# Loading and adding the expert rows of a mixture-of-experts block ahead of its last expert, whose own rows come in by a one-hot matmul

## The chip, the cores and the metric

The kernel runs on one core of a Trainium2 chip. Its time is the device time of one execution in microseconds (us). A profile of one execution stands beside it: its span runs from the first instruction to the last, and the execution's own time is a little longer.

## The reference, cut to what matters

One encoder layer: attention and pooling, an output projection, then a mixture of experts over 1024 tokens of 1024 channels, then a final norm. Each token goes to two of 32 experts, and its output is the weighted sum of their two rows.

```python
xb = x_pad[row_tok].reshape(n_blocks, MOE_BLOCK, D)
def expert_block(args):
    xblk, e = args
    hid = jax.nn.silu(xblk @ w_gate[e]) * (xblk @ w_up[e])
    return hid @ w_down[e]
yb = lax.map(expert_block, (xb, block_e)).reshape(P, D)
y = jnp.zeros((N + 1, D), jnp.float32).at[row_tok].add(yb.astype(jnp.float32) * row_w[:, None])
...
x = x + g2[:, None] * y
return rms_norm(x, final_g)
```

## The kernel before

Attention, projection, second norm and router come first; the router leaves, for every expert, up to 128 slots: `ix[:, 0, e]` holds the token of each slot, `ix[:, 1, e]` its row in a DRAM array `yd` of 2048 rows (two for each token), `LV[:, e]` its weight. Slots that no token took carry an index out of bounds and move nothing. Where an expert has more than 128 tokens, a loop under `tc.If(nr > 0)` takes the rest in further rounds; on these inputs `nr` is 0 and the loop's body is not entered.

The main loop walks over `seq`, 384 steps of one 512 KB weight tile (`we`) each. A tile is split four steps ahead (`AHEAD`) into a rounded part `wh`, written by ScalarE (ACT), and the rest `wl`, written by VectorE (DVE); PE multiplies with three products each. For expert `e`, GpSimd (POOL) gathers the tokens' rows by an indirect DMA, PE transposes them (`px`), ACT and DVE split them into `xs`; `pg` holds the gate and up products, `hx` the hidden rows, `pht` and `hth` their transpose, `py` the result. ACT evicts `py` with the weights as `y`, and POOL scatters `y` into `yd`. An expert's down products stand between the gate and up products of the next, so the last expert's end has nothing beside it.

After the loop comes the If, and after it the tail: `g2B` (the gate row, broadcast) is loaded, then 16 loads of 512 KB bring `yd` back as `fy{t}_0` and `fy{t}_1` for the eight token tiles `t`. Per tile, PE adds the two by multiplying both with the identity into `yp`; DVE multiplies with `g2B` and adds the residual `xf`; ACT squares and sums; DVE and POOL make the factor `frs`; DVE scales with `frs` and the norm's row `fgB`; and SyncE (SP) stores the tile.

The engines run their instructions in program order (`pins`). All large tiles are slabs of 4 KB a partition out of one pool of 50 (`slab`, tag "s"); a slab that is given back goes to a later tile, and what writes that tile first waits for the last use of the slab by its former owner. A ring (`ring`) takes its slabs when each of its tiles is first asked for, and keeps them. SP's loads go out in order, and each waits for the semaphore that the load eight before it raises on landing (`DMAHW0` to `DMAHW7`); POOL's have `DMASW0` to `DMASW7`.

At the If every engine that goes past the body first waits, in the branch not taken, until its own semaphores stand where the program left them before the If, and then sets them to what the body would have left. For SP these are the eight semaphores of its loads.

Of the kernel before, what the change touches and what calls it, by code (L numbers as in the profile page):

```python
# [9 lines left out]
F32 = mybir.dt.float32  # L10
# [58 lines left out]
def block_kernel(ctx: ExitStack, tc: tile.TileContext, A):  # L69
# [32 lines left out]
    def dma(dst, src):  # L102
        tc.keep_in_program_order(nc.sync.dma_start(dst, src))  # L103
# [4 lines left out]
    def pool_dma(dst, src):  # L108
        tc.keep_in_program_order(nc.gpsimd.dma_start(dst, src))
# [82 lines left out]
    xnd = dram.tile([S, D], F32, name="xnd")  # L192
    mvd = dram.tile([T, P, 2, 3, NE], F32, name="mvd")
    LV = cst.tile([P, NE], F32, name="LV")
    ix = cst.tile([P, 2, NE], I32, name="ix")

    seq = []
# [13 lines left out]
    with tc.tile_pool(name="ps0", bufs=2, space=PSUM) as psum, tc.tile_pool(name="ps1", bufs=2, space=PSUM) as psum1, \  # L211
# [9 lines left out]
        def pw(name, shape):  # L221
            return shaped(psum1.tile([P, 512], F32, name=name, tag="w"), shape)
# [19 lines left out]
        def w_split(m, eng=None):  # L242
            w = wsp[m]
            hi, lo = slab(f"wih{m}", (KD, P), F32R), slab(f"wil{m}", (KD, P), F32R)
            split(w, hi, lo, eng)
            wsp[m] = hi, lo
# [785 lines left out]

        dve.tensor_scalar(ix, lists[:, 0:64].rearrange("p (a b) -> p a b", a=2), FAR, None, op0=OP.add)
        dve.tensor_copy(LV, lists[:, 64:96])
        pn = pw("pn", (NE,))
        pe.matmul(pn, ones_b, cums[:, T], start=True, stop=True)
        most = cst.tile([P, 2], F32, name="most")
# [12 lines left out]
    with tc.tile_pool(name="ps5", bufs=2, space=PSUM) as psum, tc.tile_pool(name="ps6", bufs=4, space=PSUM) as psum1:  # L1050

        def pt(name):
            return psum.tile([P, 1024], F32, name=name, tag="p")

        def pq(name, shape=(512,)):
            t = psum1.tile([P, 512], F32, name=name, tag="q")[:, :int(np.prod(shape))]
            if len(shape) == 2:
                t = t.rearrange("p (a b) -> p a b", a=shape[0])
            return t

        def gather(dst, col):
            pool.indirect_dma_start(
                out=dst, out_offset=None, in_=xnd,
                in_offset=bass.IndirectOffsetOnAxis(ap=col, axis=0), bounds_check=S - 1, oob_is_err=False)

        SC = []

        def scatter(src, col):
            s = pool.indirect_dma_start(
                out=yd, out_offset=bass.IndirectOffsetOnAxis(ap=col, axis=0), in_=src, in_offset=None,  # L1070
                bounds_check=2 * S - 1, oob_is_err=False)
            for o in SC:
                tc.declare_no_dep(s.ins, o.ins, reason="each row is written once")
            SC.append(s)

        XF = []
        XT, PG, PU, HS, HT, PY = {}, {}, {}, {}, {}, {}
        RINGS = {}
        XG = [X2.pop(t) for t in (T - 2, T - 1)]
        X2.clear()  # L1080

        def ring(name, n, shape=(1024,), dt=F32):

            r = RINGS.setdefault(name, [[], 0])
            if len(r[0]) < n:
                r[0].append(slab(f"{name}{len(r[0])}", shape, dt))
            r[1] += 1
            return r[0][(r[1] - 1) % n]

        def w_split(e, i):  # L1090
            if i < 8 + DOWN:
                w = RW[e, i]
                hi, lo = ring("wh", WQ, dt=F32R), ring("wl", WQ, dt=F32R)
                split(w, hi, lo)
                RW[e, i] = hi, lo

        PX = {}

        def make_x(e, step):

            a, second = divmod(step, 2)
            if not second:
                p = PX[a] = pq(f"px{e}_{a}", (4, P))
                for b in range(4):
                    k = 4 * a + b
                    pe.transpose(p[:, b], XG[e % 2][:, k * P:(k + 1) * P], ident)
            else:
                x = XT[e, a] = ring("xs", 3, (2, 4, P), F32R)
                split(PX.pop(a), x[:, 0], x[:, 1])

        def products(e, i):
            w, RW[e, i] = RW[e, i], None
            if i < 8:
                hi, lo = w
                if i % 4 == 0:
                    (PG, PU)[i // 4][e] = pq(f"pg{e}_{i}")
                p = (PG, PU)[i // 4][e]
                for j in range(2):
                    k, cs = 2 * (i % 4) + j, slice(j * 512, (j + 1) * 512)
                    x = XT[e, k // 4]  # L1120
                    mm3(p, x[:, 0, k % 4], x[:, 1, k % 4], hi[:, cs], lo[:, cs], k == 0, k == KD - 1)
            else:
                k = i - 8
                if k == 0:
                    PY[e] = pt(f"py{e}")
                for h in range(2):
                    cs = slice(h * 512, (h + 1) * 512)
                    if k < DOWN:
                        mm3(PY[e][:, cs], HT[e][0][:, 0, k], HT[e][0][:, 1, k], w[0][:, cs], w[1][:, cs], k == 0, k == KF - 1)
                    else:  # L1130
                        pe.matmul(PY[e][:, cs], HT[e][1][:, k], w[:, cs], start=(k == 0), stop=(k == KF - 1))

        def hidden(e):
            dve.tensor_tensor(HS[e], HS[e], PU.pop(e), op=OP.mult)

        def hidden_t(e):
            hs = HS.pop(e)
            p = pq(f"pht{e}", (KF, P))
            for k in range(KF):
                pe.transpose(p[:, k], hs[:, k * P:(k + 1) * P], ident)  # L1140
            HT[e] = ring("hth", 1, (2, DOWN, P), F32R), DOWN < KF and ring("ht", 1, (KF, P))
            split(p[:, :DOWN], HT[e][0][:, 0], HT[e][0][:, 1])
            if DOWN < KF:
                act.activation(HT[e][1][:, DOWN:], p[:, DOWN:], AF.Copy)

        gather(XG[0], ix[:, 0, 0:1])
        gather(XG[1], ix[:, 0, 1:2])
        pool_dma(*stores.pop())
        for g in range(AHEAD):
            w_split(*seq[g])  # L1150
        for step in (0, 2, 1, 3):
            make_x(0, step)
        for g, (e, i) in enumerate(seq):
            while len(RW) < min(g + 1 + LOAD, len(seq)):
                w_next()
            if len(RW) == len(seq) and not XF:
                for t in range(T):
                    XF.append(slab(f"xf{t}"))
                    dma(XF[t], x2d[t * P:(t + 1) * P])
            if g + AHEAD < len(seq):  # L1160
                w_split(*seq[g + AHEAD])
            products(e, i)
            if i >= 8:
                e += 1
            j = i + 4 * (4 <= i < 8) - 4 * (i >= 8)
            if j == 0:
                if e > 0:
                    hidden(e - 1)
                if e + 2 < NE:
                    gather(XG[e % 2], ix[:, 0, e + 2:e + 3])  # L1170
            if j == HTJ and 0 < e < NE:
                hidden_t(e - 1)
            if j == 4 - (e == 0) and e < NE:
                HS[e] = ring("hx", 1, (512,))
                act.activation(HS[e], PG.pop(e), AF.Silu)
            if j == 8 and e > 0 or j == 7 and e == NE:
                y = ring("y", YN)
                act.activation(y, PY.pop(e - 1), AF.Copy, scale=LV[:, e - 1:e])
                scatter(y, ix[:, 1, e - 1:e])
            if j == 11 and e == NE - 1:  # L1180
                hidden(e)
                hidden_t(e)
            if e + 1 < NE and j in (X_AT if e else X_AT0):
                make_x(e + 1, (X_AT if e else X_AT0)[j])


    nr = nc.values_load(nri[0:1, 0:1], min_val=0, max_val=7)
    with tc.tile_pool(name="ps7", bufs=1, space=PSUM) as psum:
        with tc.If(nr > 0):
            with tc.For_i(0, nr):  # L1190
# [14 lines left out]
                with tc.For_i(0, NE) as e:  # L1205
# [33 lines left out]
                                             start=(k == 0), stop=(k == KF - 1))  # L1239
                    nc.scalar.activation(y, py.rearrange("p a b -> p (a b)"), AF.Copy, scale=wc)  # L1240
                    scatter(y, col[:, 1])


    g2B = slab("g2B")
    bcast_row(g2B, rowd[3:4], D)
    Y = []
    for t in range(T):
        for k in range(2):
            Y.append(slab(f"fy{t}_{k}"))
            dma(Y[-1], yd.rearrange("(t k) d -> k t d", k=2)[k, t * P:(t + 1) * P])  # L1250

    pins.update(EN)
    psum = ctx.enter_context(tc.tile_pool(name="ps8", bufs=3, space=PSUM))
    fgB = rows(psum.tile([P, D], F32, name="fgB", bufs=1), fg)
    SS, RF, YP = {}, {}, {}
    for t in range(-1, T + 2):
        if t + 1 < T:
            y0, y1 = Y[2 * t + 2:2 * t + 4]
            p = YP[t + 1] = psum.tile([P, 2, 512], F32, name=f"yp{t + 1}", tag="yp")
            for h in range(2):  # L1260
                for i, y in enumerate((y0, y1)):
                    pe.matmul(p[:, h], ident, y[:, h * 512:(h + 1) * 512], start=(i == 0), stop=(i == 1))
        if 0 <= t < T:
            y0, y1 = Y[2 * t:2 * t + 2]
            dve.tensor_tensor(y0, YP.pop(t).rearrange("p a b -> p (a b)"), g2B, op=OP.mult)
# [93 lines left out]
```

## Time and profile before

| | |
|---|---|
| time, median of 3 runs | 1163.71 us (1161.6 to 1164.07) |
| the profiled execution: its own time | 1163.77 us |
| its span | 1162.0 us |
| busy over the span | PE 94%, DVE 83%, ACT 63%, POOL 21% |
| mean granted clock of TensorE | 0.97 of full speed |

The busy shares are means over stages with different limits: the expert loop runs from about 537 to 1110 us, the tail from 1110 us on. Lines of the profile name the place in the program; a helper that records the operations gives nearly all of them line 82, so tiles are named instead. A row of the timeline gives start, duration, engine, line, operation, output<-inputs and, in brackets, how long the engine had been idle and what ended that.

### The profile page before, as it was taken

What the parts mean: (1) busy time and instruction counts of PE and PEld (TensorE: products, weight loads), DVE (VectorE), ACT (ScalarE), POOL (GpSimd) and SP (SyncE); (2) the same over time, 40 slices, a digit from 0 to 9 for tenths busy, and PEclk for the clock granted to TensorE, in tenths of its full rate; (3) what the DMA queues carried; (4) which work ended last, traced back from release to release, by engine and by line L of the source; (5) the groups of instructions that cost most, each with busy time, mean ns of one, the idle gap of its engine ahead of it and who ended that gap; (6) DMA issues with size and microseconds to landing.
All of it is one profiled execution on the core that took longest, in us unless ns stands there. A gap on an engine that the chain in (4) does not pass through costs nothing.

```text
span 1162.0 us, 15763 instructions
## 1 busy us (share of the span) xinstructions
PE 1094.0 (94%) x5319; PEld 894.8 (77%) x5319; DVE 967.5 (83%) x1222; ACT 726.8 (63%) x931; POOL 242.7 (21%) x195
## 2 busy tenths in 40 slices
PE   5998998999999999878999999999999999999975
PEld 5787786779888877777888888888888888888742
DVE  6977787589998247997999999999999999999827
ACT  6641232388887001216888888888888888888712
POOL 1000000168888001541011011110110110110001
PEclk8899999999999999969999999999999999999988
DMA  9949699696837853774999999999999999999155
GB/s 368 374 148 379 215 341 339 254 262 150 198 113 248 332 199 129 246 273 142 337 374 387 386 382 394 382 388 391 383 389 381 389 384 386 380 388 344 39 222 222
DMA packets 103718, 349.61 MB, mean 301 GB/s; under 512 B 16754, under 2 KB 17682, under 8 KB 103634
## 3 DMA queue, kind: packets, MB, share of 16 engines
q1 hardware_dynamic: 92034, 323.08, 76.4%
q0 software_dynamic: 11456, 24.96, 5.7%
q8 instruction: 43, 0.70, 0.2%
q10 hardware_dynamic: 144, 0.52, 0.1%
q14 instruction: 41, 0.34, 0.1%
HBM read 309.95 MB, written 55.33 MB: 314 GB/s over the span
## 4 chain that ended last, share of the span: by engine, by line
issue 46%; PE 27%; DVE 12%; POOL 6%; DMA 6%; ACT 1%; SPq 1%; POOLq 0%; DVEq 0%; ACTq 0%
PE pm L82 6%; PE s L82 4%; PE po L82 4%; POOL x L82 4%; PE pz_v L82 3%; PE pz_u L82 3%; POOL yd L82 2%; PE pw L82 2%; DVE rt L82 2%; DVE wt L82 2%; DMA k<-kd 1%; DVE fy L82 1%; SPq L103 1%; PE yp L82 1%; PE pz_q L82 1%
## 5 line engine op out<-in xcount | busy, mean ns | idle before, releaser
L82 DVE TENSOR_TENSOR wl<-we,wh 128x1024 fp32r<-128x1024 f32 x384 | 458.3, 1221 | 39.8 <-ACT wh L82 35.4
L82 ACT ACTIVATE wh<-we 128x1024 fp32r<-128x1024 f32 x384 | 399.7, 1058 | 60.4 <-PE pg L82 29.2
L82 PE MATMUL pg<-wh,xs 128*128 128x512 f32 x1024 | 338.7, 397 | 0.0
L82 PEld LDWEIGHTS pg<-wh,xs 128*128 128x128 f32 x1024 | 192.8, 188 | 39.2 <-ACT xs L82 0.2
L82 PE MATMUL pg<-wl,xs 128*128 128x512 f32 x512 | 200.1, 391 | 0.0
L82 PE MATMUL py<-wh,hth 128*128 128x512 f32 x512 | 171.8, 397 | 1.0 <-ACT hth L82 0.7
L82 POOL DMA_INDIRECT yd<-y,ix x32 | 32.2, 1005 | 479.5 <-ACT y L82 466.9
L82 PEld LDWEIGHTS py<-wh,hth 128*128 128x128 f32 x512 | 96.0, 188 | 21.8 <-DVE hth L82 1.2
L82 PEld LDWEIGHTS pg<-wl,xs 128*128 128x128 f32 x512 | 96.7, 189 | 18.3
L82 PE MATMUL py<-wl,hth 128*128 128x512 f32 x256 | 99.8, 390 | 0.0
L82 ACT ACTIVATE e<-s,mx 128x1024 f32<-128x1024 f32 x64 | 71.6, 1119 | 28.9 <-DVE mx L82 25.6
L82 DVE TENSOR_REDUCE mx<-s 128x1 f32<-128x1024 f32 x64 | 78.2, 1222 | 5.9 <-PE s L82 3.2
L82 PE MATMUL s<-k,sq 128*128 128x512 f32 x256 | 72.5, 405 | 5.7 <-ACT e L82 4.6
L82 POOL TENSOR_TENSOR e<-e,e 128x1024 f32<-128x1024 f32 x32 | 76.6, 2393 | 2.7
L82 PE MATMUL po<-wh,v 128*128 128x256 f32 x256 | 60.6, 301 | 0.0
L82 DVE SCALAR_TENSOR_TENSOR wt<-wt,cB 128x1024 f32<-128x1024 f32 x48 | 56.3, 1219 | 0.8 <-ACT cB L82 0.8
L82 POOL TENSOR_SCALAR e<-e,cc 128x1024 f32<-128x1024 f32 x32 | 39.3, 1228 | 83.3 <-DVE cc L82 72.2
L82 PEld LDWEIGHTS py<-wl,hth 128*128 128x128 f32 x256 | 48.2, 188 | 9.4
L82 PEld LDWEIGHTS s<-k,sq 128*128 128x128 f32 x256 | 44.0, 189 | 14.5 <-ACT e L82 7.9
L82 ACT ACTIVATE xn<-x 128x1024 f32<-128x1024 f32 x7 | 7.4, 1062 | 75.3 <-DVE x L82 64.7
L82 POOL DMA_INDIRECT x<-xnd,ix x32 | 46.2, 1442 | 35.5 <-PE px L82 13.8
L82 PE MATMUL pm<-woB,mxh 128*128 128x512 f32 x128 | 44.5, 430 | 4.4 <-DVE x L82 4.4
(236 smaller groups left out, 1842.5 us busy)
## 6 DMA issues: line engine op xcount, KB each, us to landing
we<-in_w_exp SPq DMA_DIRECT2D x384, 512.0 KB
wt<-in_w_ada SPq DMA_DIRECT2D x48, 512.0 KB
win<-in_w_in SPq DMA_DIRECT2D x16, 512.0 KB
woB<-wod SPq DMA_DIRECT2D x16, 512.0 KB
fy<-yd SPq DMA_DIRECT2D x16, 512.0 KB
k<-kd SPq DMA_DIRECT2D x32, 192.0 KB
xt<-in_xT SPq DMA_DIRECT2D x8, 512.0 KB
wo<-in_w_out SPq DMA_DIRECT2D x8, 512.0 KB
```

What stands on the lines that cost most here:

```text
L82: ins = getattr(self.eng, op)(*args, **kw)
L103: tc.keep_in_program_order(nc.sync.dma_start(dst, src))
```

## The change

The last expert's rows no longer go through `yd`. Near the start of the expert loop POOL clears a slab (`zero`) and scatters it into the last expert's rows of `yd`. The 16 loads of `yd` are issued inside the loop, during the last expert's up products, behind the scatter of the last expert but one, and DVE adds the two rows of a token tile (`first_sum`): three tiles before the last expert's down products in program order, five in the tail. POOL makes a one-hot `OH` of 128 slots by 1024 tokens, and PE adds `OH` times the last `y` to the identity product of the sum. In the If's body the loads and three sums are made again. `g2B` is still loaded after the If.

```diff
+        dve.tensor_scalar(tlast, lists[:, NE - 1:NE], FAR, None, op0=OP.add)
...
+        def sums_load(h):
+
+            t, k = divmod(h, 2)
+            if len(Y) < 2 * T:
+                Y.append(slab(f"fy{t}_{k}"))
+            dma(Y[h], yd.rearrange("(t k) d -> k t d", k=2)[k, t * P:(t + 1) * P])
+
+        def first_sum(t):
+            dve.tensor_tensor(Y[2 * t], Y[2 * t], Y[2 * t + 1], op=OP.add)
+
         gather(XG[0], ix[:, 0, 0:1])
         gather(XG[1], ix[:, 0, 1:2])
         pool_dma(*stores.pop())
+        zero = slab("zero")
+        pool.memset(zero, 0.0)
+        scatter(zero, ix[:, 1, NE - 1:NE])
+        del zero
...
+            if i == 8 and e == NE - 1:
+                for t in range(3):
+                    first_sum(t)
...
-                scatter(y, ix[:, 1, e - 1:e])
+                if e < NE:
+                    scatter(y, ix[:, 1, e - 1:e])
+                else:
+                    ylast = y
+            if j == 9 and e == NE - 1:
+
+                OH.append(slab("onehot"))
+                pool.iota(OH[0], pattern=[[1, S]], base=0, channel_multiplier=0, allow_small_or_imprecise_dtypes=True)
+                pool.tensor_scalar(OH[0], OH[0], tlast, None, op0=OP.is_equal)
+                for h in range(2 * T):
+                    sums_load(h)
...
     g2B = slab("g2B")
     bcast_row(g2B, rowd[3:4], D)
-    Y = []
-    for t in range(T):
-        for k in range(2):
-            Y.append(slab(f"fy{t}_{k}"))
-            dma(Y[-1], yd.rearrange("(t k) d -> k t d", k=2)[k, t * P:(t + 1) * P])
...
     for t in range(-1, T + 2):
+        if 3 <= t + 2 < T:
+            first_sum(t + 2)
         if t + 1 < T:
-            y0, y1 = Y[2 * t + 2:2 * t + 4]
             p = YP[t + 1] = psum.tile([P, 2, 512], F32, name=f"yp{t + 1}", tag="yp")
             for h in range(2):
-                for i, y in enumerate((y0, y1)):
-                    pe.matmul(p[:, h], ident, y[:, h * 512:(h + 1) * 512], start=(i == 0), stop=(i == 1))
+                cs = slice(h * 512, (h + 1) * 512)
+                pe.matmul(p[:, h], ident, Y[2 * t + 2][:, cs], start=True, stop=False)
+                pe.matmul(p[:, h], OH[0][:, (t + 1) * P:(t + 2) * P], ylast[:, cs], start=False, stop=True)
```

How the instructions move is shown at three places. The first is ACT at the start of the expert loop, where it writes the first rounded weights and the first rounded token rows (`xs0`, `xs1`; the numbers behind the names count tiles, and brackets give the semaphores waited for). Before:

```order
L82 ACTIVATE wh0_4709<-we0_0_3960 128x1024 [waits DMAHW4_49,DMAHW3_49]
L82 ACTIVATE wh1_4713<-we0_1_3962 128x1024 [waits DMAHW5_49,DMASW6_49,Pool_49]
L82 ACTIVATE wh2_4717<-we0_2_3972 128x1024 [waits DMAHW6_49,DVE_49,Activation_49]
L82 ACTIVATE wh3_4721<-we0_3_3974 128x1024 [waits DMAHW0_49,DMAHW7_49,DMASW0_49,PE_49]
L82 ACTIVATE xs0_4735<-px0_0_4725 128x512 [waits DVE_49,PE_49]
L82 ACTIVATE xs1_4738<-px0_1_4730 128x512 [waits DVE_49,PE_49]
L82 ACTIVATE wh4_4741<-we0_4_3984 128x1024 [waits DVE_49]
```

And with the change:

```order
L82 ACTIVATE wh0_4716<-we0_0_3961 128x1024 [waits DMAHW5_49,DMAHW4_49,Pool_49]
L82 ACTIVATE wh1_4720<-we0_1_3963 128x1024 [waits DMAHW2_49,Activation_49]
L82 ACTIVATE wh2_4724<-we0_2_3973 128x1024 [waits DMAHW1_49,DMAHW6_49,DVE_49,PE_49]
L82 ACTIVATE wh3_4728<-we0_3_3975 128x1024 [waits DMAHW7_49,DMASW1_49,Activation_49]
L82 ACTIVATE xs0_4742<-px0_0_4732 128x512 [waits DVE_49,PE_49]
L82 ACTIVATE xs1_4745<-px0_1_4737 128x512 [waits DVE_49,PE_49]
L82 ACTIVATE wh4_4748<-we0_4_3985 128x1024 [waits DMAHW0_49,DVE_49]
```

The order is the same, but `zero` took a slab of the pool, so the rings' tiles fall on other slabs: `wh3` now waits for `DMASW1`, which stands for POOL's store of `mv` to `mvd` (`pool_dma(*stores.pop())`, line 109), the last user of its slab. Before, that wait stood on DVE at `wl4`, behind both `xs`. With the change `wl4` waits for `DMASW3`, the landing of `zero`'s scatter.

The second place is SP from the last `xf` load on. Before, these rows stand behind the If, whose branch not taken ends with the first of them:

```order
L1189 UNCONDITIONAL_BRANCH [waits DMAHW0_49,DMAHW1_49,DMAHW2_49,DMAHW3_49,DMAHW4_49,DMAHW5_49,DMAHW6_49,DMAHW7_49]
L103 DMA g2B_9723<-rowd_115 128x1024 [waits DMAHW1_49,DVE_49]
L103 DMA fy0_0_9725<-yd_117 128x1024 [waits DMASW7_49,DMAHW2_49,DMASW1_49,PE_49]
L103 DMA fy0_1_9727<-yd_117 128x1024 [waits DMAHW3_49,DVE_49]
L103 DMA fy1_0_9729<-yd_117 128x1024 [waits DMAHW4_49,PE_49]
```

With the change, ahead of the If (the first five of the 16 loads) and behind it:

```order
L103 DMA xf7_9274<-x2d_116 128x1024 [waits DMAHW0_49,DMASW5_49,DVE_49]
L103 DMA fy0_0_9509<-yd_117 128x1024 [waits DMAHW1_49,DMASW7_49,DVE_49]
L103 DMA fy0_1_9511<-yd_117 128x1024 [waits DMAHW2_49,DVE_49]
L103 DMA fy1_0_9513<-yd_117 128x1024 [waits DMAHW3_49,DVE_49]
L103 DMA fy1_1_9515<-yd_117 128x1024 [waits DMAHW4_49,DVE_49]
L103 DMA fy2_0_9517<-yd_117 128x1024 [waits DMAHW5_49,DVE_49]
```

```order
L1220 UNCONDITIONAL_BRANCH
L1220 UNCONDITIONAL_BRANCH [waits DMAHW0_49,DMAHW1_49,DMAHW2_49,DMAHW3_49,DMAHW4_49,DMAHW5_49,DMAHW6_49,DMAHW7_49]
L103 DMA g2B_9784<-rowd_115 128x1024 [waits DMAHW1_49,DVE_49,PE_49]
L103 DMA out<-fy0_1_9511 128x1024 [waits DMAHW2_49,DVE_49]
L103 DMA out<-fy1_1_9515 128x1024 [waits DMAHW3_49,DVE_49]
```

The 16 loads moved ahead of the If, and the load of `g2B` stayed behind it, so it now follows them in SP's order, behind the branch that waits for the eight semaphores of SP's loads. `DMASW7` at the first load is now the scatter of the last expert but one.

The third place is DVE in the tail, at token tiles 0 to 2. Before:

```order
L82 TENSOR_TENSOR fy0_0_9725<-yp0_9769,g2B_9723 128x1024 [waits DMAHW1_49,DVE_49,DMAHW2_49,PE_49,Activation_49]
L82 TENSOR_TENSOR fy0_0_9725<-fy0_0_9725,xf0_9253 128x1024 [waits DVE_49]
L82 TENSOR_TENSOR fy1_0_9729<-yp1_9774,g2B_9723 128x1024 [waits DMAHW4_49,PE_49]
L82 TENSOR_TENSOR fy1_0_9729<-fy1_0_9729,xf1_9255 128x1024 [waits DVE_49]
L82 TENSOR_SCALAR fr_m_9793<-fss_9781 128x1 [waits Activation_49]
L82 TENSOR_TENSOR fy2_0_9733<-yp2_9783,g2B_9723 128x1024 [waits DMAHW6_49,PE_49]
```

With the change:

```order
L82 TENSOR_TENSOR fy0_0_9509<-yp0_9798,g2B_9784 128x1024 [waits DVE_49,DMAHW1_49,PE_49,Activation_49]
L82 TENSOR_TENSOR fy0_0_9509<-fy0_0_9509,xf0_9260 128x1024 [waits DVE_49]
L82 TENSOR_TENSOR fy3_0_9521<-fy3_0_9521,fy3_1_9523 128x1024 [waits DMAHW6_49,DMAHW5_49,DMAHW7_49,DMAHW0_49,DMASW4_49]
L82 TENSOR_TENSOR fy1_0_9513<-yp1_9803,g2B_9784 128x1024 [waits PE_49]
L82 TENSOR_TENSOR fy1_0_9513<-fy1_0_9513,xf1_9262 128x1024 [waits DVE_49]
L82 TENSOR_SCALAR fr_m_9823<-fss_9810 128x1 [waits Activation_49]
L82 TENSOR_TENSOR fy4_0_9525<-fy4_0_9525,fy4_1_9527 128x1024 [waits DMAHW7_49,DMAHW2_49,DMAHW0_49]
```

The sums of tiles 3 to 7 stand between the products with `g2B`, behind the first of them.

## Rows read from the trace of the kernel before

**Rows 1.** Windows: stretch and length, engines' busy time, TensorE clock, DMA share, GB/s.

```profile
537.00:1100.00 563.00, 562.65 (x2651) 464.64 (x2652) 523.05 (x505) 482.63 (x538) 75.23 (x61) 1.00 0.94 358
...
537.00:539.00 2.00, 2.00 (x6) 1.52 (x7) 1.59 (x3) 1.49 (x2) 1.05 (x1) 0.52 0.16 34
```

**Rows 2.** The chain that ended last: start, duration, what it waited for.

```profile
1111.02 4.41 DMA yd<-y,ix
1115.57 3.84 DMA fy<-yd
```

**Rows 3.** Timeline of the end of the expert loop and the start of the tail.

```profile
1096.04 0.33 SPq L103 DMA_DIRECT2D g2B<-rowd  x1
...
1097.39 0.98 POOL L82 DMA_INDIRECT yd<-y,ix  x1 [16.29 <-ACT y L82]
...
1109.63 1.11 ACT L82 ACTIVATE y<-py,LV 128x1024 f32<-128x1024 f32 x1 [6.10 <-PE py L82]
...
1110.84 2.05 PE L82 MATMUL fgB<-ident,cols 128*128 128x128 f32 x16 [1.25 <-ACTq L1189]
1111.02 0.98 POOL L82 DMA_INDIRECT yd<-y,ix  x1 [12.65 <-ACTq L1189]
1115.57 14.30 SPq L103 DMA_DIRECT2D fy<-yd  x16
...
1119.45 29.28 PE L82 MATMUL yp<-fy,ident 128*128 128x512 f32 x64 [6.56 <-DMA fy<-yd]
...
1124.79 1.22 DVE L82 TENSOR_TENSOR fy<-yp,g2B 128x1024 f32<-128x1024 f32 x1 [20.54 <-PE yp L82]
```

**Rows 4.** Timeline of DVE in the tail: one token tile, and the last scaling.

```profile
1138.90 1.22 DVE L82 TENSOR_TENSOR fy<-yp,g2B 128x1024 f32<-128x1024 f32 x1
1140.15 1.22 DVE L82 TENSOR_TENSOR fy<-fy,xf 128x1024 f32<-128x1024 f32 x1
...
1141.36 1.27 DVE L82 SCALAR_TENSOR_TENSOR fy<-fy,frs,fgB 128x1024 f32<-128x1024 f32 x1
1142.55 1.22 DVE L82 TENSOR_TENSOR fy<-yp,g2B 128x1024 f32<-128x1024 f32 x1
...
1153.74 2.46 DVE L82 SCALAR_TENSOR_TENSOR fy<-fy,frs,fgB 128x1024 f32<-128x1024 f32 x2
```

**Rows 5.** The tile view of yd from 1040 us on: issue to landing of five scatters.

```profile
DMA to landing us min/median/max: 3.2/4.4/7.0
```

**Rows 6.** Windows of the DMA engines: behind the scatter of 1097.39, and during the loads.

```profile
1100.60:1102.60 2.00, 0.36 (x3) 0.36 (x4) 1.59 (x2) 0.00 (x0) 0.00 (x0) 1.00 0.00 0
...
1117.50:1139.90 22.40, 20.45 (x44) 8.99 (x45) 13.19 (x14) 4.59 (x8) 1.67 (x3) 0.89 1.00 390
```

**Rows 7.** Timeline of SP: the last two of the 16 loads.

```profile
1128.27 0.32 SPq L103 DMA_DIRECT2D fy<-yd  x1
...
1129.55 0.32 SPq L103 DMA_DIRECT2D fy<-yd  x1
```

**Rows 8.** The page's costliest groups: a POOL operation on 1024 columns.

```profile
L82 POOL TENSOR_SCALAR e<-e,cc 128x1024 f32<-128x1024 f32 x32 | 39.3, 1228 | 83.3 <-DVE cc L82 72.2 <-ACT wh L82 5.2 <-ACT osq L82 3.7
```

**Rows 9.** Timeline of the start of the expert loop.

```profile
527.69 2.00 ACT L82 ACTIVATE wh<-we 128x1024 fp32r<-128x1024 f32 x2 [2.30 <-DVE pk L82]
...
533.06 0.85 POOL L109 DMA_DIRECT2D mvd<-mv  x1
...
536.09 0.60 ACT L82 ACTIVATE xs<-px 128x512 fp32r<-128x512 f32 x1 [6.40 <-PE px L82]
...
536.72 0.69 DVE L82 TENSOR_TENSOR xs<-px,xs 128x512 fp32r<-128x512 f32 x1 [1.15 <-ACT xs L82]
...
536.74 0.79 PE L82 MATMUL pg<-wh,xs 128*128 128x512 f32 x1
...
538.52 1.23 DVE L82 TENSOR_TENSOR wl<-we,wh 128x1024 fp32r<-128x1024 f32 x1 [0.25 <-ACT wh L82]
```

**Rows 10.** The tile view of mv from 500 to 545 us: issue to landing of POOL's store.

```profile
DMA to landing us min/median/max: 5.3/5.3/5.3
```

More of the change, by code (lines that the diff above doesn't have):

```diff
@@ L194, in block_kernel @@
     LV = cst.tile([P, NE], F32, name="LV")
+    tlast = cst.tile([P, 1], F32, name="tlast")
     ix = cst.tile([P, 2, NE], I32, name="ix")
@@ L1074, in scatter @@
             SC.append(s)
-        XF = []
+        XF, Y, OH = [], [], []
         XT, PG, PU, HS, HT, PY = {}, {}, {}, {}, {}, {}
@@ L1184, in block_kernel @@
                 make_x(e + 1, (X_AT if e else X_AT0)[j])
+        RINGS.clear()
     nr = nc.values_load(nri[0:1, 0:1], min_val=0, max_val=7)
@@ L1241, in block_kernel @@
                     scatter(y, col[:, 1])
+            for h in range(2 * T):
+                sums_load(h)
+            for t in range(3):
+                first_sum(t)
     g2B = slab("g2B")
     bcast_row(g2B, rowd[3:4], D)
-    Y = []
-    for t in range(T):
-        for k in range(2):
-            Y.append(slab(f"fy{t}_{k}"))
-            dma(Y[-1], yd.rearrange("(t k) d -> k t d", k=2)[k, t * P:(t + 1) * P])
     pins.update(EN)
```

## The prediction

> **What bounds the kernel now.** I read the windows over the whole expert loop first. From 537 to 1100 us PE is busy for 562.65 of 563 us at full clock [rows 1]: in this stage PE alone sets the time, so what starts its first product later by so much ends the loop later by as much. Then the end of the chain: the last scatter takes 4.41 us to land, and only then does SP load `yd` back, of which the first load takes 3.84 us until PE can use it [rows 2]. The timeline shows what lies around this: the last `y` is done at 1110.74 (1109.63 + 1.11), the loads are issued from 1115.57 on, PE's first sum starts at 1119.45, and DVE's first product with `g2B` at 1124.79, after 20.54 us of idleness [rows 3]. From there DVE sets the pace: one token tile costs it 3.65 us (1142.55 - 1138.90), back to back, for a product, an addition and a scaling of 1.2 us each [rows 4]. DVE's tail runs from 1124.79 to 1156.20 (1153.74 + 2.46), 31.4 us, of which eight tiles of 3.65 are 29.2; the rest is PE's slow start and the last tile's norm. The last store ends 5.8 us later with the span, 1162.0.
>
> The change goes for the stretch from 1110.7 to 1124.8. What it does there, and what it does where nobody looks, at the loop's start, I cost apart.
>
> **The loads.** The first one waits for the scatter of the last expert but one, issued at 1097.39 [rows 3]. Scatters land 3.2 to 7.0 us after issue [rows 5]; this one's traffic is over by 1100.6, since the engines are empty from there [rows 6], so 3.2 holds, and the first load goes out at about 1100.75 (the last scatter landed at 1115.43, and SP issued at 1115.57: 0.14 later). That is 14.8 us earlier than before. The slabs of `fy` do not hold it: their last users are splits of weights done by 1097.
>
> How long do 16 loads take? The 16th was issued at 1129.55, when the eighth had landed, so the eighth landed 14.0 us after the first issue; the issues were then 1.28 us apart [rows 7], which is the pace of landing. Eight more make 24.2 us from first issue to last landing. The DMA engines were full in that stretch (share 1.00, 390 GB/s) [rows 6], so there is no faster pace to be had from an earlier start. The last load lands at 1100.75 + 24.2 = 1124.95. The Trainium skill prices this otherwise: the page "DMA: Bandwidth & Descriptors", section "Anatomy of one DMA — SWDGE (gpsimd) path", has about 2.0 us plus the bytes over 436 GB/s, an estimate of 21.2 us for 8.39 MB as one stream, which would make the whole sum 1172.8. The trace has 24.2 for the same bytes, and that is used.
>
> **g2B.** Its load was issued at 1096.04, long before it was needed [rows 3]. Now it stands behind the If, and in the branch not taken SP waits for all eight semaphores of its loads, that is for the 16th to land. So `g2B` goes out at 1125.1. Alone in the queue it needs between 3.2 us (the fastest scatter [rows 5]) and 3.84 (the first load [rows 2]); I take 3.5, so 1128.6. DVE's first product in the tail waits for it, and behind that product, in DVE's order, stand five sums and everything else. So this wait, and not the rows of `yd`, starts the tail: 3.8 us later than 1124.79.
>
> **The sums.** Three lie in DVE's idle time: the sixth load lands two paces before the eighth, at 1100.75 + 11.4 = 1112.2, and the third sum ends at 1113.4. PE's `fgB`, which began at 1110.84, comes behind them after the If (PE waits for DVE's count there), so at 1113.5. With 2.05 us for it and 29.28/8 = 3.66 for a tile [rows 3], the first `yp` is done at 1119.2, and at half the clock by 1125: in both cases before `g2B`. The one-hot costs PE nothing, since it takes the place of the second identity product. The other five sums are new work on the bound engine, 5 x 1.22 = 6.1 us. In return the tail's slow start goes, since three `yp` wait for DVE: 29.2 + 6.1 + 0.3 for the last norm (my share of the 2.2 us by which 31.4 exceeds 29.2) = 35.6 instead of 31.4, so +4.2. Together the end costs 3.8 + 4.2 = **+8.0 us**.
>
> **The one-hot and the cleared rows on POOL.** Two operations and a memset on 1024 columns. The trace has one such operation at 1.23 us [rows 8]; the iota and the memset have no row at this size, and lie between nothing and that. POOL is idle for 12.65 us ahead of its last scatter [rows 3], so they are hidden; without that cover they would cost at most 2.5 us, and would still be done before `g2B` lands.
>
> **The loop's start.** `zero` takes a slab, and the rings move to others. `wh3` gets the slab of `mv` and waits for POOL's store of it, issued at 533.06 [rows 9] and landed 5.3 us later, at 538.4 [rows 10]. Before, `wl4` waited for that landing, and hardly: it ran at 538.52 [rows 9]. On ACT both `xs` are queued behind `wh3`, and PE waits for them. ACT wrote the first `xs` at 536.09; now it follows `wh3` by half of the 2.00 us of two splits, at 539.4, so +3.3. The remainder of `xs` on DVE is queued behind `wl3`, which waits for `wh3` too: 538.4 + 1.0 + 1.2 = 540.6 against 536.72, so +3.9 [rows 9]. PE's third product needs it. PE was at half clock in its first products (0.52 at 537 to 539) [rows 1]; it now idles once more in front of them, so that phase may last longer, by up to 1 us. I take **+4.0 us**, between 3.3 and 5.0. `wl4` waits for the zeros to land, about 3.2 to 4.4 us behind a POOL issue near 538.6, so to 543 at most, while PE wants it some 5.5 us (four weight tiles) after 540; if that landing took 7 us it would add about 1. As PE never waits later in the loop, nothing takes these 4 us back.
>
> **Sum.** 1163.77 (the profiled execution; the median is 1163.71, the same) + 4.0 + 8.0 = **1175.8 us**, 1.0% slower.
>
> **Rivals.**
> - The start's wait is absorbed (0.12): ACT or the loads catch up. For it speaks that ACT is idle for 80 of 563 us in the loop; against it that PE is not [rows 1]. Then 1163.8 + 8.0 = 1171.8.
> - SP does not wait at the branch (0.08). `g2B` is then still the 17th load in the queue, and lands one pace behind the 16th, at 1126.2: 1163.8 + 4.0 + 1.4 + 4.2 = 1173.4. Against it stands the branch's row, with eight semaphores.
> - Not slower (0.05): the loads run faster beside the last expert than they did in the tail. Their price is 1.28 us each. The tail can't start before the first `yp` at 1119.2; if `g2B` is there by then, the start is 5.6 us earlier than before instead of 3.8 later, and the sum is 1175.8 - 9.4 = 1166.4, at the edge of no change. This needs 16 loads in 14.8 us (1119.2 - 3.6 - 1100.75), 0.93 us each or 567 GB/s, where full engines moved 390 [rows 6]; from 0.93 downward it decides.
> - The change doesn't do what it says (0.03): a slab or a semaphore keeps the loads back until 1115 as before. Then `g2B` lands at 1143.5, and the time is about 1163.8 + 4 + 18.7 + 4.2 = 1190.7. Against it: each of their waits is on work done by 1101.
>
> **Numbers.** My forecast has 0.72. The likeliest case reaches from 1172 (a start of 3.3, a quicker `g2B`, and the loads gaining 3 us) to 1180 (a start of 5, a scatter that lands after 7.0 us instead of 3.2). Down to the case without the start's cost, with a margin, the range is 1170 to 1180; it leaves out part of the two last rivals and little else. About 0.2% (2.3 us) can be told from no change here; by the cases, with the third rival divided between them: faster 0.02, same 0.03, slower 0.95.
>
> **What would show it.** In the trace of the changed kernel: the first `pg` product about 3.3 us later than 536.74, behind ACT's `wh` that ends near 539.4; the last `y` some 4 us later than before; the `fy` loads issued about 9 us ahead of that `y`; DMA full for 24 us and then one load of 512 KB by itself; DVE's first product with `g2B` not ahead of that load's landing, some 18 us behind `y`, although `yp` was done; and DVE then without a gap for about 35 us, at 4.9 us a tile where it holds a sum. I am wrong if PE starts `pg` as before, if `g2B` is issued before the last `fy` has landed, or if DVE's tail begins with `yp`'s end.

## The result, and the profile after

The changed kernel takes 1177.08 us (median of 4 runs, 1176.18 to 1180.77) where the kernel before takes 1163.89 (4 runs, 1161.6 to 1164.61): a ratio of 1.0124, 95% interval 1.0103 to 1.0145, so 1.2% slower. The forecast was 1175.8, with a range of 1170 to 1180.

The profiled execution of the changed kernel is its longest run: 1180.77 us, span 1179.0. Part of its excess is not the change's. POOL's store of `mv`, behind which the change begins, is issued at 536.64, and at 533.06 before [rows 9]: 3.6 us of difference had gathered by then, under code that the change leaves as it was but for a `tlast` of 0.15 us on DVE. The traces of all kernels here have this store between 529.5 and 536.6, so stretches are counted from it, or from a row near the stretch. From the store to the end of the span it is 642.4 us now and 628.9 before: 13.4 us more, as the medians say (13.2).

The timeline of the changed kernel at the start of the loop, to be read beside [rows 9] (`SPq`, `ACTq` and `DVEq` in the rows are the sequencers of these engines, which wait, branch and issue DMAs):

```profile
533.65 1.06 ACT L82 ACTIVATE wh<-we 128x1024 fp32r<-128x1024 f32 x1 [1.73 <-PE pn L82]
...
536.64 0.85 POOL L109 DMA_DIRECT2D mvd<-mv  x1
537.48 0.98 POOL L82 MEMSET zero<- 128x1024 f32 x1
...
538.71 1.07 PE L82 MATMUL px<-ident,x 128*128 128x128 f32 x8 [2.98 <-DMA x<-xnd,ix]
...
542.16 1.06 ACT L82 ACTIVATE wh<-we 128x1024 fp32r<-128x1024 f32 x1 [7.45 <-DMA mvd<-mv]
543.12 1.07 ACT L82 ACTIVATE xs<-px 128x512 fp32r<-128x512 f32 x2
...
543.76 0.80 PE L82 MATMUL pg<-wh,xs 128*128 128x512 f32 x1 [3.97 <-ACT xs L82]
```

ACT stands for 7.45 us in front of the fourth `wh` until the store of `mv` lands, 5.5 us after its issue; both `xs` are behind it, and PE idles. The first `pg` comes 7.12 us after the store's issue, in the kernel before 3.68: 3.4 us later.

Windows of the changed kernel, and then of the kernel before, each from its first `pg` on (columns as in [rows 1]; the engines are PE, PE's weight loads, DVE, ACT and POOL):

```profile
543.70:549.90 6.20, 5.99 (x13) 4.30 (x14) 4.42 (x5) 2.71 (x5) 0.00 (x0) 0.50 0.10 40
549.90:552.00 2.10, 2.10 (x10) 1.65 (x9) 1.11 (x1) 1.60 (x2) 0.00 (x0) 0.98 0.00 0
```

```profile
536.70:538.90 2.20, 2.20 (x6) 1.73 (x6) 1.76 (x3) 1.54 (x2) 1.05 (x1) 0.50 0.06 21
538.90:542.90 4.00, 4.00 (x19) 3.24 (x18) 3.06 (x3) 2.84 (x3) 0.00 (x0) 1.00 0.23 58
```

The granted clock is 0.50, the lower of its two levels (1.2 GHz), for 6.2 us after the longer idleness, and for 2.2 before. At half the clock, half of the 4.0 us more is lost, 2.0.

The timeline of the changed kernel from the last scatter to the tail, beside [rows 3]:

```profile
1105.67 0.98 POOL L82 DMA_INDIRECT yd<-y,ix  x1 [16.27 <-ACT y L82]
...
1107.79 4.73 POOL L82 TENSOR_SCALAR onehot<-onehot,tlast 128x1024 f32<-128x1024 f32 x1
1108.91 14.70 SPq L103 DMA_DIRECT2D fy<-yd  x16
...
1119.51 1.11 ACT L82 ACTIVATE y<-py,LV 128x1024 f32<-128x1024 f32 x1 [7.70 <-PE py L82]
1120.80 1.23 DVE L82 TENSOR_TENSOR fy<-fy,fy 128x1024 f32<-128x1024 f32 x1 [1.87 <-DMA fy<-yd]
1122.22 2.64 PE L82 MATMUL fgB<-ident,cols 128*128 128x128 f32 x16 [2.76 <-DVEq L1220]
...
1128.33 1.02 PE L82 MATMUL yp<-y,onehot 128*128 128x512 f32 x2
...
1134.32 0.33 SPq L103 DMA_DIRECT2D g2B<-rowd  x1
1138.18 1.23 DVE L82 TENSOR_TENSOR fy<-yp,g2B 128x1024 f32<-128x1024 f32 x1 [16.16 <-DMA g2B<-rowd]
...
1170.76 2.47 DVE L82 SCALAR_TENSOR_TENSOR fy<-fy,frs,fgB 128x1024 f32<-128x1024 f32 x2
```

The loads go out 10.6 us ahead of the last `y`, and PE has done the first `yp` by 1129.35 (1128.33 + 1.02, the last product of its second half), but DVE idles 16.16 us until `g2B` lands. Windows of the same kernel around this:

```profile
1109.00:1133.50 24.50, 19.54 (x63) 12.26 (x64) 5.83 (x6) 1.71 (x2) 3.52 (x1) 0.86 0.92 345
1133.70:1134.30 0.60, 0.60 (x2) 0.19 (x1) 0.00 (x0) 0.00 (x0) 0.00 (x0) 1.00 0.00 0
1134.30:1138.00 3.70, 1.92 (x5) 0.57 (x3) 0.00 (x0) 0.00 (x0) 0.00 (x0) 1.00 0.45 142
```

The DMA engines carry the 16 loads until about 1133.2. At the If SP's wait for the last of them ends at 1133.6, 24.7 us behind the first issue; it steps through its eight semaphores and issues `g2B` 0.7 us later, and the engines carry that load alone. SP at the line of the If, with the first and the last start:

```profile
L1220 SPq EVENT_SEMAPHORE  x8: 17/17/17, 1133.6 to 1134.2; - x8
```

One tile of the tail that holds a sum (DVE's timeline, beside [rows 4]) lasts 4.78 us:

```profile
1150.09 1.22 DVE L82 TENSOR_TENSOR fy<-yp,g2B 128x1024 f32<-128x1024 f32 x1
1151.34 1.23 DVE L82 TENSOR_TENSOR fy<-fy,xf 128x1024 f32<-128x1024 f32 x1
...
1152.55 1.27 DVE L82 SCALAR_TENSOR_TENSOR fy<-fy,frs,fgB 128x1024 f32<-128x1024 f32 x1
1153.73 1.22 DVE L82 TENSOR_TENSOR fy<-fy,fy 128x1024 f32<-128x1024 f32 x1
1154.87 1.22 DVE L82 TENSOR_TENSOR fy<-yp,g2B 128x1024 f32<-128x1024 f32 x1
```

### The profile page after: what moved, and what is told of

Same layout as the page of the kernel before. It is cut to its first block, busy times and chain, and to the rows that moved or that the text cites. A ratio compares the mean times of both kernels' runs of the same rounds, so it can differ in the third digit from the quotient of the medians.

```text
span 1179.0 us, 15774 instructions
## 1 busy us (share of the span) xinstructions
PE 1103.1 (94%) x5319; PEld 901.1 (76%) x5319; DVE 976.5 (83%) x1231; ACT 727.0 (62%) x931; POOL 250.5 (21%) x198
## 5 line engine op out<-in xcount | busy, mean ns | idle before, releaser
L82 ACT ACTIVATE e<-s,mx 128x1024 f32<-128x1024 f32 x64 | 71.7, 1121 | 28.9 <-DVE mx L82 24.7
L82 DVE SCALAR_TENSOR_TENSOR x<-pm,Y,x 128x1024 f32<-128x1024 f32 (+1 forms) x33 | 41.2, 1249 | 8.4 <-PE pm L82 6.7
```

Source lines behind the costliest of these rows:

```text
L82: ins = getattr(self.eng, op)(*args, **kw)
```

## The experiments

Each ratio is to runs of the kernel before on the same chip; their medians there were 1162.4 to 1164.3. The start of the tail is given as the time from the start of the last `y` to DVE's first product with `g2B`: 15.16 before [rows 3], 18.67 in the changed kernel. That `y` itself comes 13.6 us behind the `y` before it where the clock does not fall in the last expert, and up to 16.3 where it does (see the last experiment). Where two versions differ in this, another point to count from is named.

**g2B ahead of the loads.**

```diff
             if j == 9 and e == NE - 1:
...
+                g2B = slab("g2B")
+                bcast_row(g2B, rowd[3:4], D)
                 for h in range(2 * T):
                     sums_load(h)
...
-    g2B = slab("g2B")
-    bcast_row(g2B, rowd[3:4], D)
```

> The changed kernel with g2B's slab and load moved ahead of the sixteen loads of yd; all else stays. Theory of the prediction (the tail waits for g2B, which waits for the 16th load and the branch): g2B lands before the rows, DVE's tail starts when the first yp is done (1127.4 in the changed kernel's trace) instead of 1138.2, 10.8 us earlier, so 1177.1 - 10.8 = 1166.3 us; up to 2 more if PE at half clock makes the tail's first tiles slow, 1168.3. Rival: another wait at the If or on the rows of yd keeps the tail back; then the time stays within 1.5 us of 1177.

Measured: 1169.67 us, ratio 1.0052 (1.0028 to 1.0076), 0.7% under the changed kernel. Its timeline:

```profile
1105.48 14.89 SPq L103 DMA_DIRECT2D fy<-yd  x16
...
1114.47 1.11 ACT L82 ACTIVATE y<-py,LV 128x1024 f32<-128x1024 f32 x1 [6.10 <-PE py L82]
...
1118.90 3.75 PE L82 MATMUL fgB<-ident,cols 128*128 128x128 f32 x16 [4.47 <-DVEq L1222]
...
1126.63 1.23 DVE L82 TENSOR_TENSOR fy<-yp,g2B 128x1024 f32<-128x1024 f32 x1 [7.94 <-PE yp L82]
...
1130.26 1.06 ACT L82 ACTIVATE fy<-fy 128x1024 f32<-128x1024 f32 x1 [14.67 <-SPq L1222]
1130.76 1.23 DVE L82 TENSOR_TENSOR fy<-fy,fy 128x1024 f32<-128x1024 f32 x1 [1.64 <-SPq L1222]
```

With `g2B` there, `yp` starts the tail: 12.16 us behind `y` instead of 18.67, and, as `y` comes 1.6 us earlier here, 21.15 behind the first load's issue instead of 29.27, which is 8.1 us earlier. The theory holds, but of its 10.8 us only 6.3 are left at the end (636.0 us from the store of `mv` to the end of the span, 642.4 in the changed kernel). 2.0 were a misreading of mine: I put the first `yp` at 1127.4, when its second half was still to come, and it was done at 1129.35. Another 0.7 goes since `fgB`, which waits in both for DVE to pass the If behind its third sum, runs at half the clock here (3.75 us, 2.64 in the changed kernel). And behind the first tile ACT and DVE now wait for SP, which is still at the branch (`SPq L1222`), 1.64 us for DVE. The rival was half right: the If does keep work back.

**g2B still 17th, but ahead of the If.** Its two lines stand behind the 16 `sums_load` in the loop.

> The changed kernel with g2B's load still behind the sixteen loads, but issued ahead of the If, so that SP does not wait at the branch before it. Theory (the branch's wait plus a load alone in the queue cost 0.7 + 3.7 us behind the 16th landing): g2B lands one pace of 1.3 us behind the 16th instead of 4.4 behind it, so the tail starts 3.1 us earlier: 1177.1 - 3.1 = 1174.0 us. Rival: the place in the queue alone sets it, and the branch costs nothing; then 1177, within 1 us.

Measured: 1175.05 us, ratio 1.0100 (1.0069 to 1.0130), 0.24% under the changed kernel, which the intervals don't tell from none. The trace does: the tail starts 15.55 us behind `y`, 3.1 earlier, as the theory said, and by as much counted from the first load (26.14 instead of 29.27). So this is what it costs `g2B` to stand behind the branch: SP's 0.7 us there and a load by itself, instead of one pace more. The row names SP, but SP gets past the branch only when `g2B`, now the last load, has landed:

```profile
1106.97 15.00 SPq L103 DMA_DIRECT2D fy<-yd  x16
...
1133.11 1.23 DVE L82 TENSOR_TENSOR fy<-yp,g2B 128x1024 f32<-128x1024 f32 x1 [12.74 <-SPq L1222]
```

**The cleared rows later.** Slab, memset and scatter move behind the first products of expert 0; the same bytes are written.

```diff
-        zero = slab("zero")
-        pool.memset(zero, 0.0)
-        scatter(zero, ix[:, 1, NE - 1:NE])
-        del zero
...
                     gather(XG[e % 2], ix[:, 0, e + 2:e + 3])
+                if e == 0:
+                    zero = slab("zero")
+                    pool.memset(zero, 0.0)
+                    scatter(zero, ix[:, 1, NE - 1:NE])
+                    del zero
```

> The changed kernel with the cleared rows moved: slab, memset and scatter come behind the first products of expert 0, so that the rings take the slabs that they had before, and the same bytes are still written. Theory (the shift of the slabs makes ACT's wh wait for the store of mv): the first pg product starts as early behind the lists as before, the first y is 5.6 us earlier than in the changed kernel, and the time is 1177.1 - 5.2 = 1171.9 us (1171 to 1173). Rival (the memset and the scatter themselves, on POOL and the DMA engines, delay the loop): the time stays within 1 us of 1177. Rival (the wait is absorbed later in the loop): also 1177.

Measured: 1169.87 us, ratio 1.0056 (1.0035 to 1.0076), 0.7% under the changed kernel. The time lies below the 1171 to 1173 expected; 5.2 us are 0.45%, within what the two intervals leave open, and from the store to the end of the span the trace has 5.4 us less (636.9). The first `pg` comes 3.35 us behind the store's issue at 532.68, as before; ACT writes `xs` when `px` is there:

```profile
532.68 0.84 POOL L109 DMA_DIRECT2D mvd<-mv  x1
...
535.38 1.09 ACT L82 ACTIVATE xs<-px 128x512 fp32r<-128x512 f32 x2 [6.12 <-PE px L82]
...
536.03 0.72 PE L82 MATMUL pg<-wh,xs 128*128 128x512 f32 x1 [0.25 <-ACT xs L82]
```

It is the shift of the slabs, not the clearing, that costs the start: with the clearing near the loop's start, ACT waits for the store of `mv` and not for the zeros. A shift without any clearing was not run.

**The start's part alone**, in the kernel before; the zeros go to a spare buffer.

```diff
+    spare = dram.tile([P, D], F32, name="spare")
...
         pool_dma(*stores.pop())
+        zero = slab("zero")
+        pool.memset(zero, 0.0)
+        pool_dma(spare, zero)
+        del zero
```

> The kernel before with only the start's part of the change: a cleared slab at the same place, stored by POOL to a spare buffer instead of scattered into yd; the end is untouched. Theory: wh of the fourth weight tile waits for the store of mv, the first product comes 3.5 us later and runs longer at half clock; 1163.9 + 5.2 = 1169.1 us (1168 to 1170). Rival (the start's wait is absorbed): 1163.9, within 1 us.

Measured: 1167.32 us, ratio 1.0045 (1.0032 to 1.0059), which is 5.2 us on 1163.9, the theory's figure (3.7 to 6.9 by the interval; the time itself lies below the 1168 to 1170 expected). From the store to the end of the span it is 5.7 us more than before. The same wait stands in its timeline:

```profile
534.83 1.06 ACT L82 ACTIVATE wh<-we 128x1024 fp32r<-128x1024 f32 x1 [7.18 <-DMA mvd<-mv]
...
536.42 0.29 PEld L82 LDWEIGHTS pg<-wh,xs 128*128 128x128 f32 x1 [3.22 <-ACT xs L82]
```

**Both repairs** (g2B first and the cleared rows late).

> The changed kernel with g2B's load first and the cleared rows late, both repairs together. If the two costs add: the start as in the kernel before, the tail 12.2 us behind the last y's start instead of 15.2 before and 18.7 in the changed kernel, but 5.4 us longer than before by its sums and by a wait of 1.6 us at the If: about 1164.5 us (1162.5 to 1167), no better than before. Rival (the start's wait and the tail's overlap, so that they don't add): 1169.7, as with g2B first alone.

Measured: 1165.45 us, ratio 1.0025 (1.0008 to 1.0041): with both costs gone the change is still no gain. That the two add is seen in the traces: from the store to the end of the span both repairs take away 11.7 us (630.7), the two by themselves 6.3 and 5.4. The ratios are too wide for it (1.0% together, 0.7% each). The tail starts 7.48 us behind `y`, which comes late here (16.3 us behind the one before), but then waits for SP at the If. DVE's row of this wait begins 25.3 us behind the first load's issue, as with `g2B` first alone:

```profile
1120.26 1.22 DVE L82 TENSOR_TENSOR fy<-yp,g2B 128x1024 f32<-128x1024 f32 x1 [5.76 <-PE yp L82]
...
1126.47 1.23 DVE L82 TENSOR_TENSOR fy<-fy,fy 128x1024 f32<-128x1024 f32 x1 [3.73 <-SPq L1223]
```

**PE adds everything.** Both repairs, all `first_sum` left out, one product more per half:

```diff
                 pe.matmul(p[:, h], ident, Y[2 * t + 2][:, cs], start=True, stop=False)
+                pe.matmul(p[:, h], ident, Y[2 * t + 3][:, cs], start=False, stop=False)
                 pe.matmul(p[:, h], OH[0][:, (t + 1) * P:(t + 2) * P], ylast[:, cs], start=False, stop=True)
```

> Both repairs, and all of DVE's sums left out: PE adds both rows of each token and the last expert's y in three products. Theory formed after the first runs (behind the If, whoever uses a loaded row waits for SP to pass the branch, and SP passes it when all sixteen loads have landed, some 15.7 us behind the last y's start): the first yp product starts 16 us behind y, the tail 18 us behind it, with 30.1 us instead of 35.5 to its last scaling: 1164.8 us (1163 to 1167), the sums' gain eaten by the wait. Rival (each row is waited for by its own landing): the tail starts 7.5 us behind y: 1154.5 us.

Measured: 1180.08 us, ratio 1.0162 (1.0144 to 1.0179), worse than either theory. The wait at the If is as the first said:

```profile
1108.05 2.05 PE L82 MATMUL fgB<-ident,cols 128*128 128x128 f32 x16 [1.25 <-ACTq L1220]
1121.17 3.78 PE L82 MATMUL yp<-fy,ident 128*128 128x512 f32 x4 [11.07 <-SPq L1220]
```

The tail lasts 42.4 us from DVE's first product to its last scaling, where both had 30.1: they had PE's price wrong, as the next two runs show.

**Six and four loads ahead of the If.** As the last, with six (then four) loads in the loop and the others behind the If.

> As the kernel in which PE adds all rows, with only the first six loads ahead of the If and ten behind it. Theory (the branch waits for the loads that cross it): SP passes it when the sixth load has landed, 3.6 us behind the last y's start, fgB follows, the tail starts 8.5 to 10 us behind y instead of 18: 1157 us (1155 to 1160), faster than the kernel before. Rival (the wait is not for the loads that cross, or PE's third product per half sets the pace): within 2 us of the version with sixteen ahead.

> The same with four loads ahead of the If and twelve behind it. Theory: the fourth load lands 0.3 us behind the last y's start, so the branch costs nothing, fgB runs beside y's scaling, and the tail starts some 5 to 6 us behind y: 1153.5 us (1151 to 1157). Rival (the loads behind the If come too late for DVE's tail): the tail shows gaps and the time is that of six loads ahead or more.

Measured: 1168.89 us, ratio 1.0064 (1.0045 to 1.0083), and 1170.56, ratio 1.0073 (1.0056 to 1.0090). The theory of the branch holds: the tail starts 8.51 us behind `y`, in both, and no row waits for SP. (With four ahead 5 to 6 were expected.) But DVE then waits for PE (six ahead; the 15.11 us in front of the tail are put down to a load that landed then, but PE's first tile was done only at that moment, and with four ahead this row names PE):

```profile
1118.83 1.88 PE L82 MATMUL yp<-fy,ident 128*128 128x512 f32 x4
1119.09 1.23 DVE L82 TENSOR_TENSOR fy<-yp,g2B 128x1024 f32<-128x1024 f32 x1 [15.11 <-DMA fy<-yd]
...
1120.55 1.02 PE L82 MATMUL yp<-y,onehot 128*128 128x512 f32 x2
...
1124.18 1.23 DVE L82 TENSOR_TENSOR fy<-yp,g2B 128x1024 f32<-128x1024 f32 x1 [2.61 <-PE yp L82]
```

A half tile of three products takes PE 2.58 us (1118.83 to 1121.41, where the next begins), a tile 5.15; [rows 3] have 3.66 for two per half. So PE, and not DVE, sets the pace, as the rival had it for the third product; its number (within 2 us of sixteen ahead) does not hold: the two versions are 11.2 and 9.5 us faster than that one, as their tails start earlier. That the late loads hold DVE back is refuted: it works at PE's pace of 5.15 us a tile in both. I had set a product at half its price, each being two records of 0.43 us.

**Sums again, on POOL or DVE.** Four loads ahead with two sums on DVE before the If, twelve behind it; PE has two products per half. The other six sums are on POOL, or on DVE:

```diff
+    def next_sum(t):
+        if t < T:
+            pool.tensor_tensor(Y[2 * t], Y[2 * t], Y[2 * t + 1], op=OP.add)
+
+    next_sum(2)
...
             rsqrt(RF[t - 1], SS[t - 1], 1, 1.0 / D, "fr")
+        if t >= 0:
+            next_sum(t + 3)
```

> Four loads ahead of the If with their two sums on DVE before the If, twelve loads behind it with their six sums on POOL; PE adds one summed row block and the last expert's y (two products per half, as before); g2B first, cleared rows late. Theory (PE at three products per half set the pace of 5.15 us a tile; with two it is 3.43, below DVE's 3.65, and POOL's sums of 2.4 us lie beside both): the tail starts 6.6 us behind y instead of 15.2 in the kernel before, with its 30.1 us: 8.6 us earlier, and with 0.9 us from the loop and up to 2.6 lost where PE falls to half clock in the last expert: 1154.8 us (1152.5 to 1157.5). Rival (POOL's sums slow DVE beside them, or come too late): DVE's operations grow above 1.22 us or gaps open; up to 7 us more, 1162.

> The same with the six later sums on DVE instead of POOL. Theory (every sum in the tail costs DVE 1.22 us, since DVE sets its pace): 6 x 1.22 = 7.3 us more than with POOL, tail 37.4 us to its last scaling, 1162.1 us (1160 to 1164). Rival (DVE waits in the tail anyway, so that its sums fill gaps): within 2 us of the version with POOL.

Measured: with POOL 1156.74 us, ratio 0.9959 (0.9939 to 0.9979); with DVE 1159.48, ratio 0.9961 (0.9946 to 0.9976). Both beat the kernel before, by 0.4%. The tail starts 6.79 us behind `y` in both. As this `y` comes 14.7 and 15.0 us behind the one before it, and 13.6 in the kernel before, the gain is not the whole 8.4 us: counted from the `y` before, the tail starts 7.2 and 6.9 earlier. With POOL, the last two `y`, the start of the tail, and DVE and POOL beside each other in it:

```profile
1093.97 1.10 ACT L82 ACTIVATE y<-py,LV 128x1024 f32<-128x1024 f32 x1
...
1108.70 1.11 ACT L82 ACTIVATE y<-py,LV 128x1024 f32<-128x1024 f32 x1 [7.21 <-PE py L82]
...
1115.49 1.22 DVE L82 TENSOR_TENSOR fy<-yp,g2B 128x1024 f32<-128x1024 f32 x1 [6.92 <-PE yp L82]
...
1126.16 2.37 POOL L82 TENSOR_TENSOR fy<-fy,fy 128x1024 f32<-128x1024 f32 x1
1126.67 1.21 DVE L82 TENSOR_TENSOR fy<-yp,g2B 128x1024 f32<-128x1024 f32 x1
1127.91 1.69 DVE L82 TENSOR_TENSOR fy<-fy,xf 128x1024 f32<-128x1024 f32 x1
...
1130.78 1.21 DVE L82 TENSOR_TENSOR fy<-yp,g2B 128x1024 f32<-128x1024 f32 x1
```

DVE's addition takes 1.69 us beside POOL's sum (1.22 without), and a tile 4.11 instead of 3.65, so both theories of the first version are partly right. It looks like a wait: in the four tiles where the two meet, DVE's addition ends 1.07 or 1.08 us behind the end of POOL's (here 1129.60 and 1128.53), however early it began. From its first product to the last scaling the tail lasts 33.55 us with POOL and 35.03 with DVE, against 31.4 before [rows 3, 4]. The 7.3 us by which DVE's version was to be longer are refuted: by the traces it is 1.5 in the tail and 2.0 from the store to the end of the span (625.1 and 623.1, before 628.9). POOL's version has 33.55 where 30.1 was expected, and in DVE's the first of the six sums lies ahead of the tail. The rival's number (within 2 us) holds, but not its reason, as this tail is without gaps. By their ratios the two versions can't be told apart.

**PE kept busy in the last expert.** The version with POOL's sums and sixteen products of the identity that nobody reads: twelve ahead of `pht`, four behind it.

> The version with four loads ahead of the If and POOL's sums, with sixteen products of the identity that nobody reads in PE's idle time of the last expert (twelve while it waits for DVE's hx, four while it waits for hth). Theory (PE's granted clock falls in the last expert because PE idles there; the last two y then lie 14.7 to 16.3 us apart instead of 13.6): they lie 13.6 us apart in this trace, and the time falls by 1 to 2.6 us: 1155 us (1153.5 to 1156.5). Rival (the clock falls whatever PE does, or the products delay the last expert's own): 14.5 us or more, and 1156.7 or slower.

Measured: 1159.15 us, ratio 0.9959 (0.9942 to 0.9976), as without them. The clock is 1.00 in the window that begins with the last down products, where it was 0.68 without them:

```profile
1104.50:1108.50 4.00, 4.00 (x21) 3.08 (x20) 1.92 (x2) 0.31 (x1) 0.34 (x1) 1.00 0.98 363
```

```profile
1102.00:1106.00 4.00, 4.00 (x13) 3.11 (x13) 1.44 (x2) 0.00 (x0) 0.19 (x1) 0.68 0.98 362
```

But the products take 2.84 us, in a gap of 1.79, and hold the last expert back; the last two `y` lie 14.3 us apart, 13.6 where the clock did not fall. From the store to the end of the span it is 623.0 us, as without them (623.1). In three executions without the products (the kernel before, g2B first, PE adds everything) the clock did not fall either, so one trace does not settle that idleness is the cause. It stays open.

## Why the prediction was right

In the traces it is +13.4 us where +12.0 was forecast. Step by step the forecast misses by +0.7 at the start, -0.1 and +0.5 at the loads, +0.5 and +0.4 at `g2B` and -0.6 in the tail: the sum is right because its terms are, and no large errors cancel. Only at the start do two misses offset each other, a longer time at half the clock and a loop that gave 0.9 us back, which nothing in the prediction foresaw.

- **The loop's start, +4.0.** The first `pg` is 3.4 us later (forecast 3.3) for the cause named. The time at half the clock was sized too small in it: at most 1 us forecast, 2.0 found, so the first scatter of a `y` is 5.6 us later, counted from the store (573.93 against 564.80). At the scatter of the last expert but one 4.7 are left; the loop itself gave back 0.9, on which see below. `wl4` did not have to wait for the zeros.
- **The loads, 24.2 us.** First load 3.24 us behind the scatter (forecast 3.36). From its issue to the 16th landing it took 24.7 us. The Trainium skill's price (page "DMA: Bandwidth & Descriptors", section "Anatomy of one DMA — SWDGE (gpsimd) path"), which is for a single DMA issued by GpSimd and gave an estimate of 21.2 us in the prediction, is 3.5 us too short for these 16 of SP's; the pace of the trace before was the better price.
- **g2B behind the branch.** SP's issue came 0.7 us behind the 16th landing (forecast 0.15), DVE's first product 3.9 later (3.5). From the first load's issue to that product it was 29.3 us, forecast 27.85. The second run takes the branch from in front of `g2B` and gains 3.1.
- **The sums.** The tail lasts 35.05 us from DVE's first product, forecast 35.6. A tile with a sum is 4.78, forecast 4.9.
- **POOL's work hidden.** True, but mis-sized: comparing for the one-hot took 4.73 us, not 1.23 [rows 8]; it was done at 1112.52, 8 us before the end of the last `y`, with which PE uses it.
- **The last y 4 us later.** 6.3 from the store: the clock fell in the last expert's down products (the last two `y` 15.2 us apart, 13.6 before). It cost nothing here, as `g2B` decided.

Of the rivals, the absorbed start is refuted by the fourth run (+5.2 us alone), the branch without a wait by SP's 0.7 us with empty DMA engines and by the second run. That the loads run faster beside the last expert is refuted by their 24.7 us. The loads did go out early, so the rival that the change does not do what it says falls too.

The prediction saw that the If keeps back `g2B`, and not that it keeps back every engine: whoever needs, behind the If, a row that was loaded ahead of it waits for SP, and SP for the loads that are still under way. In the changed kernel `g2B` hid this. It shows as soon as `g2B` is early (1.64 us, 3.73, 11.07).

## What to carry to other kernels

A transfer that is started ahead of such an If is waited for at its branch, by the engine that issued it and through it by all that need what it loaded: send ahead only what will have landed when the branch is reached, and leave small loads that the code behind needs in front of the long ones. Work that takes a buffer out of a shared pool in front of a tuned start can cost more by the buffers that others get than by what it does; the same clearing 6 us later, with its scatter 3 us later, cost nothing that the start shows. And a sum that moves off one engine has to be priced on the next at the rate its trace shows, with what it does to its neighbours.

## What the runs showed of the hardware that was not expected

- POOL's `is_equal` of 128 x 1024 against a column took 4.72 to 4.74 us in all eleven traces that have it, four times the 1.23 of its other operation with a scalar in [rows 8]. DVE's splits of weights run beside its first 2.1 us (in the changed kernel until 1109.87); whether a part of it is waiting for them is not shown.
- DVE's addition of two slabs goes from 1.22 to between 1.68 and 1.87 us beside an addition on POOL, and ends 1.07 to 1.09 us behind it each time (eight times, in the two versions with POOL's sums), as if it waited for POOL's to end; its product out of PSUM (1.21) does not change. The other way round, POOL's addition that began 0.18 us behind one of DVE's took 3.27 us instead of 2.35 (at 1116.93, in the first of these versions).
- The loop runs faster by about 0.9 us, from first to 31st scatter 531.7 us (573.93 to 1105.67) in the changed kernel and 532.6 in the kernel before (564.80 to 1097.39) and in the one with the start's part alone (565.86 to 1098.49). So it goes with the part of the change at the end and not with the start's; the cause is not known.
